# Last group of the FFN down projections as eight plain block products, with the folding of sums, the second down's memory and the first mixer chunk rearranged

## The chip, the cores and the metric

The kernel runs on one core of a Trainium2 chip. It computes one whole decoder layer in one launch. The metric is the device time of that launch in microseconds, as the median of several runs. Engines are called as the profile calls them: PE (TensorE, the matmuls), PEld (its weight loads), DVE (VectorE), ACT (ScalarE), POOL (GpSimd), SP (SyncE, which here only issues DMAs).

## What is computed

The reference is a layer with two half-step feed-forward networks (FFN) around a mixer, cut here to what matters:

```python
def swiglu(x, w_gate, w_up, w_down):
    return (jax.nn.silu(x @ w_gate) * (x @ w_up)) @ w_down

def half_ffn(h, g_pre, g_post, w_gate, w_up, w_down):
    return h + 0.5 * rms_norm(swiglu(rms_norm(h, g_pre), w_gate, w_up, w_down), g_post)
...
h = half_ffn(h, ...)                      # FFN 1
u = rms_norm(h, g_mix_pre); u @ w_in      # mixer: DeltaNet, sliding-window attention, gates
h = h + rms_norm(y @ w_out, g_mix_post)
h = half_ffn(h, ...)                      # FFN 2
```

The model width is 1024, the hidden width 2816 (22 tiles of 128). There are 1040 prompt tokens with the meta tokens and 64 sample tokens: FFN 1 runs over 1104 tokens, FFN 2 over 1088, so half the tokens are 552 and 544. All is in 32-bit floats.

## The kernel before

**Products.** Every float is split into a high and a low part that TensorE can multiply (`hi` and `lo`, in the names `wh`/`wl` and `xh`/`xl`), and a product is three matmuls: high by high, high by low, low by high (the list `FAST`). The two FFNs also use Strassen's scheme in Winograd's form: each of the three matrices is cut in 2 by 2 blocks (tokens in two halves, width in two halves, hidden width in two halves), and seven products of sums of blocks, p = 1 to 7, stand for the eight plain block products.

**Up.** For each pair of hidden tiles f = 0 to 10 (one of each hidden half) gate and up are computed in seven products; `hidden` (L337 to L373) makes from them the silu-gated values `h11, h12, h21, h22` and their sums, splits them, and stores seven slices per f in DRAM (`hid`, by `store`, L369).

**Down** (`Ffn.down`, L445 to L518). The pairs f are taken in groups (0,1), (2,3,4), (5,6), (7,8), (9,10). For each group the four blocks of the weight are loaded (`raw`, L244; ten buffers). For each product p: the operand of the weight is put together by up to two differences on DVE (`T`, L251 and L261) and split by an ACT cast (`wh`, L272) and a POOL subtraction (`wl`, L273), four buffers each; the slice p of `hid` of each f is loaded by SP (`hb`, L480, five buffers); and for each of the four blocks d of 128 output columns PE runs n x 3 x 2 matmuls (n the group's size, 2 the two parts of the tokens, 256 and 296 or 288 columns) into one PSUM buffer `y` (L504), which DVE adds to the accumulator `acc{p}` (L451). For the first group ACT copies it there (L508). There are four PSUM buffers, and two in the last stretch, where the other two are given to the transposes.

**The sums.** The seven accumulators are folded into the four output blocks in the last group: 6+=1, 2+=1, 3+=6, 3+=5, 7+=6, 4+=7, 5+=7, on DVE (L451) and POOL (L452) in turn with the products. Products 7 and 4 come last, in two token parts each. In FFN 1 (`early`) they are done for the last two groups in separate visits at the very end.

**Ends.** `end` (L521, L527) transposes 128 tokens t of the folded blocks to rows: `acc2` and `acc3` for t = 0 to 3, `acc4` and `acc5` for t = 4 to 7, t = 8 being the rest of both. Behind it stands the post norm (L564, L565, with the reciprocal root on POOL, L80, L81) and, in FFN 1, the mixer's pre norm (L96, L98) with its transposes (L102) and their evacuation (L117, L118) to the tiles `uT` of the mixer; in FFN 2 the norm and the store of the output. The ends are woven between the last products, and in FFN 1 also into the mixer's first projections (`m.before`: beta and decay by `ba_steps`, the keys of two heads by `keys_conv`, L745). The mixer's tokens come in chunks of 512, 256 and 336.

**Order.** The code names tiles from pools; a scheduler orders the instructions of each engine by when it expects them to be ready, and each engine then runs its own list in order, waiting on semaphores. SP's list holds nearly all DMAs, so a DMA that waits holds back those listed behind it. A new pool can lie in memory that an earlier one used, and then its first writes wait for the earlier one's last readers. So the memory of the second down (L1958 to L1965, opened after up's pools were closed) decides when its first loads can start.

## Time and profile before

| | |
|---|---|
| Median of 3 runs | 2834.3 us (2832.69 to 2837.92) |
| Profiled execution's own time | 2832.25 us |
| Its span (first to last instruction) | 2830.5 us |
| Mean granted TensorE clock | 0.978 |
| PE busy | 2660.1 us (94%), 18797 instructions |
| PEld busy | 2482.9 us (88%) |
| DVE, ACT, POOL busy | 1657.9, 1106.2, 1417.6 us (59%, 39%, 50%) |
| DMA | 422.55 MB, mean 149 GB/s |

Busy times are shares of the span, averaged over stages that are bound by different things. The stages of this execution, in microseconds from the span's start: first FFN's up until about 517, its down until about 814, the mixer and the merge until about 2135, second FFN's up until 2530.5, its down until 2814, and a tail until 2830.5. A row of the windows view gives for a stretch of time the busy time and the instructions of each engine, the granted clock of TensorE as a share of full speed, and the busy share of the DMA engines. A row of the waits view gives an engine, the operation that waited, what released it, and the total, the number and the longest of such waits.

### The profile page before, as it was taken

How to read it: one execution, taken by the hardware profiler on the slowest of the kernel's cores; microseconds unless marked ns; L12 is line 12 of the kernel's file. 1: busy time of each engine (PE TensorE's matmuls, PEld its weight loads, DVE VectorE, ACT ScalarE, POOL GpSimd, SP SyncE). 2: the span in 40 equal slices, each digit the busy share in tenths (PEclk: the TensorE clock that was granted, in tenths of full speed). 3: DMA queues.
4: the chain of work that ended last, by engine and by line, in shares of the span. 5: the costliest groups of instructions: out<-in, count | busy, mean ns of one | idle time of the engine just before them, and what ended most of it. 6: DMA issues, size and time to landing. Idle time of an engine off the chain costs nothing. (4 is left out here: it accounts for less than half of the span.)

```text
span 2830.5 us, 49313 instructions
## 1 busy us (share of the span) xinstructions
PE 2660.1 (94%) x18797; PEld 2482.9 (88%) x18797; DVE 1657.9 (59%) x2457; ACT 1106.2 (39%) x2599; POOL 1417.6 (50%) x1332
## 2 busy tenths in 40 slices
PE   7999999899878998999999999998999999979996
PEld 6999999899867897887788888887799999979996
DVE  7657656445856669955454444443566665653567
ACT  5334333322255632354444444444533433424122
POOL 6555555444765634644344444444555555544346
PEclk9999999999999999999999999999999999999998
DMA  4344343667743653353333333334434443347664
GB/s 155 130 143 158 126 148 135 244 206 246 240 154 111 216 171 98 95 178 112 91 94 94 94 94 94 94 103 135 157 98 161 146 150 133 144 166 245 224 221 166
DMA packets 234450, 422.55 MB, mean 149 GB/s; under 512 B 60278, under 2 KB 121878, under 8 KB 233926
## 3 DMA queue, kind: packets, MB, share of 16 engines
q1 hardware_dynamic: 213622, 339.72, 37.0%
q10 hardware_dynamic: 20592, 79.68, 7.1%
q8 instruction: 148, 2.42, 0.4%
q14 instruction: 88, 0.72, 0.1%
HBM read 273.71 MB, written 147.27 MB: 149 GB/s over the span
## 5 line engine op out<-in xcount | busy, mean ns | idle before, releaser
L273 POOL TENSOR_TENSOR wl<-T,wh 128x512 fp32r<-128x512 f32 x264 | 351.3, 1340 | 353.6 <-ACT wh L272 181.7
L130 PE MATMUL gu<-xh,wl 128*128 128x256 f32 (+3 forms) x1440 | 496.0, 344 | 0.0
L126 PE MATMUL gu<-xh,wh 128*128 128x256 f32 (+3 forms) x1440 | 491.9, 342 | 0.0
L128 PE MATMUL gu<-xl,wh 128*128 128x256 f32 (+3 forms) x1440 | 491.1, 341 | 0.0
L504 PE MATMUL y<-hb,wh 128*128 128x256 f32 (+2 forms) x2464 | 428.6, 295 | 51.8 <-ACT wh L272 20.3
L273 POOL TENSOR_TENSOR wl<-raw,wh 128x512 fp32r<-128x512 f32 x194 | 266.3, 1380 | 305.5 <-ACT wh L272 219.4
L504 PEld LDWEIGHTS y<-hb,wh 128*128 128x128 f32 x2464 | 362.8, 192 | 58.1 <-ACT wh L272 20.7
L272 ACT CAST wh<-T 128x512 fp32r<-128x512 f32 x264 | 163.2, 620 | 411.4 <-PE y L504 151.8
L130 PEld LDWEIGHTS gu<-xh,wl 128*128 128x128 f32 x1440 | 275.1, 191 | 28.7 <-issue 11.1
L128 PEld LDWEIGHTS gu<-xl,wh 128*128 128x128 f32 x1440 | 275.2, 191 | 20.1 <-issue 1.2
L126 PEld LDWEIGHTS gu<-xh,wh 128*128 128x128 f32 x1440 | 275.7, 191 | 19.1 <-issue 1.6
L504 PE MATMUL y<-hb,wl 128*128 128x256 f32 (+2 forms) x1232 | 266.2, 293 | 9.8 <-POOL wl L273 9.7
L451 DVE TENSOR_TENSOR acc<-acc,y 128x552 f32<-128x552 f32 (+4 forms) x240 | 161.6, 682 | 168.8 <-PE y L504 168.7
L272 ACT CAST wh<-raw 128x512 fp32r<-128x512 f32 x194 | 119.9, 620 | 326.6 <-PE y L504 130.7
L717 POOL TENSOR_TENSOR wl<-raw,wh 128x1024 fp32r<-128x1024 f32 x60 | 145.0, 2416 | 142.7 <-ACT wh L716 121.2
L504 PEld LDWEIGHTS y<-hb,wl 128*128 128x128 f32 x1232 | 205.0, 193 | 11.2 <-POOL wl L273 11.2
L251 DVE TENSOR_TENSOR T<-raw,raw 128x512 f32<-128x512 f32 x136 | 137.1, 1015 | 90.9 <-POOL wl L273 79.3
L261 DVE TENSOR_TENSOR T<-raw,T 128x512 f32<-128x512 f32 x66 | 79.7, 1214 | 79.4 <-POOL wl L273 79.4
L1478 POOL TENSOR_TENSOR f<-f,mhalf 128x1 f32<-128x1 f32 (+1 forms) x72 | 54.6, 758 | 110.9 <-DVE f L1476 103.5
L251 DVE TENSOR_TENSOR T<-raw,T 128x512 f32<-128x512 f32 x70 | 76.5, 1097 | 34.8 <-POOL wl L273 34.6
L869 DVE SCALAR_TENSOR_TENSOR cv<-pc,cw,cv 128x1131 f32<-128x1131 f32 x48 | 69.1, 1442 | 34.2 <-POOL cv L866 33.9
L363 ACT CAST hs<-S 128x552 fp32r<-128x552 f32 (+1 forms) x60 | 39.1, 652 | 116.2 <-DVE S L351 67.0
(585 smaller groups left out, 7489.5 us busy)
## 6 DMA issues: line engine op xcount, KB each, us to landing
hb<-hid SPq DMA_DIRECT2D x77, 552.0 KB
hb<-hid SPq DMA_DIRECT2D x77, 544.0 KB
hid<-hs ACTq DMA_DIRECT2D x70, 552.0 KB
hid<-hs ACTq DMA_DIRECT2D x70, 544.0 KB
raw<-in_w_in_dram SPq DMA_DIRECT2D x58, 512.0 KB
raw<-in_ffn_w_down_dram SPq DMA_DIRECT2D x104, 256.0 KB
raw<-in_ffn_w_gate_dram SPq DMA_DIRECT2D x94, 256.0 KB
raw<-in_ffn_w_up_dram SPq DMA_DIRECT2D x94, 256.0 KB
```

The lines of the kernel that those rows point to most:

```text
L126: nc.tensor.matmul(ps, wh, xh, start=first and i == 0, stop=False)
L128: nc.tensor.matmul(ps, wh, xl, start=False, stop=False)
L130: nc.tensor.matmul(ps, wl, xh, start=False, stop=last and i == n - 1)
L251: self.nc.vector.tensor_tensor(out=b[name], in0=b[x], in1=b[y], op=ALU.subtract)
L261: nc.vector.tensor_tensor(out=s, in0=b["21"], in1=s, op=ALU.subtract)
L272: nc.scalar.copy(hi, s)
L273: nc.gpsimd.tensor_tensor(out=lo, in0=s, in1=f32(hi), op=ALU.subtract)
L451: dve = lambda out, x, y: nc.vector.tensor_tensor(out=out, in0=x, in1=y, op=ALU.add)
L504: nc.tensor.matmul(self.view(ps, (i,)), w[j][x][:, d * P:(d + 1) * P], hb[j][:, y, lo:hi], start=j + x + y == 0, stop=j == n - 1 and x == 1)
L717: nc.gpsimd.tensor_tensor(out=lo, in0=raw, in1=f32(hi), op=ALU.subtract)
L869: nc.vector.scalar_tensor_tensor(out=cv, in0=pc[:, w:w + PADW], scalar=self.cw[:, j, w:w + 1], in1=cv, op0=ALU.mult, op1=ALU.add)
L1478: nc.gpsimd.tensor_tensor(out=f[rows], in0=f[rows], in1=c.mhalf[rows, 0:1], op=ALU.pow)
```

## The change

1. The last group (9,10) is no longer done in seven products but as eight plain block products: output block q of 2, 3, 4, 5 is the sum over four pairs of a plain weight block and a plain slice of `hid` (2 hidden halves, 2 pairs f). The values `h21` become an eighth slice for f = 9 and 10. The four weight blocks of both pairs are split once and kept in `w` and a new pool `w2` (four buffers each). There are no separate visits for products 7 and 4 in FFN 1 any more.
2. The sums of accumulators are issued by `beside` ahead of the plain blocks, in the order of the list `adds`; `acc2` and `acc3` are final first, so that the ends of t = 0 to 3 can run while the blocks of q = 4 and 5 run in token parts.
3. In every group of three, and in one place of the last group, the blocks d = 2 and 3 run together in one turn: each operand is used for both before the next.
4. The load and the cast of the small weights `ba` move from ahead of the first down to behind its second group, by `late_load`.
5. The first two slices that `hidden` stores for each f go through ACT's queue.
6. The mixer's first chunk is projected in two pieces of 256 columns by `ba_steps` and the first two `keys_conv`; the ends are dealt out anew (three streams in `m.before`); chunks 0, 1 and 2 of `uT` have a pool each.
7. The second down's pools are laid out anew, with the raw weights first in the order of loads, six `hb` buffers, and an unused gap; the second up's `x` tiles get a pool per product so that memory comes free product by product.

The core of the diff:

```diff
+    def values(self, hbp, group, p):
+        hb = [self.c.t(hbp, [P, 2, self.half], F32R, tag="hb") for _ in group]
+        for x, f in zip(hb, group):
+            self.nc.sync.dma_start(f32(x), self.h_d[f, p - 1].rearrange("p (x t) -> p x t", x=2))
+        return hb
+
+    def turns(self, ds, items, parts):
+        ps = {}
+        for d in ds:
+            self.psy.append(self.psy.pop(0))
+            ps[d] = self.c.t(self.psy[-1], [P, 1024], tag="y")
+        for j, (w, hb) in enumerate(items):
+            for d in ds:
+                for x, y in FAST:
+                    for i in parts:
+                        lo, hi = self.parts[i]
+                        self.nc.tensor.matmul(self.view(ps[d], (i,)), w[x][:, d * P:(d + 1) * P], hb[:, y, lo:hi],
+                                              start=j + x + y == 0, stop=j == len(items) - 1 and x == 1)
+        for d in ds:
+            yield d, self.view(ps[d], parts)
...
+                for ds in ((0,), (1,), (2, 3)) if len(group) > 2 else ((0,), (1,), (2,), (3,)):
+                    for d, v in self.turns(ds, items, both):
...
+        group = groups[-1]
+        b = self.raw("d", group, ("11", "21", "12", "22"))
+        first = [self.values(hbp, group, p) for p in (1, 2)]
+        w = {name: [self.w_split(self.wp if name[1] == "1" else self.wp2, x[name]) for x in b]
+             for name in ("11", "21", "12", "22")}
+        adds = [[(pool, 6, 1), (dve, 2, 1)], [(dve, 3, 5), (pool, 7, 6)], [(dve, 3, 6)], [(pool, 4, 7)], [(dve, 5, 7)], [], [],
+                []]
...
+        def block(q, column, hb, ds, parts):
+            items = [(x, y) for row, h in zip("12", hb) for x, y in zip(w[row + column], h)]
+            for d, v in self.turns(ds, items, parts):
+                dve(part(q, d, parts), part(q, d, parts), v)
+                yield
...
+        second = [self.values(hbp, group, p) for p in (8, 4)]
+        beside(4)
+        for i in range(2):
+            for q, column in ((4, "1"), (5, "2")):
+                for ds in ((0, 1), (2,), (3,)) if i == 0 and q == 4 else ((0,), (1,), (2,), (3,)):
+                    yield from block(q, column, second, ds, (i,))
...
+        if f in self.plain:
+            split(8, h21)
...
-    c.nc.sync.dma_start(raw, I["w_ba"])
+    late_load(c, raw, I["w_ba"])
...
-        dn = f1.down(GROUPS, accp, hbp, True)
-        drain(steps_of(dn, 28 * len(GROUPS) - 26))
+        dn = f1.down(GROUPS, [(accp, (1, 2, 5, 7, 3, 6, 4))], hbp)
+        drain(steps_of(dn, 28 * 2))
+        ba_w = ba_weights(c, nrm, I)
+        drain(steps_of(dn, 28 * 2))
...
-        weave((steps_of(dn, 8), 0, 1, 8), ends(0, 1))
-        weave((dn, 0, 1, 17), ends((0,), 2, (0,), (1,), 3, (1,), (2,), 4, (2,), (3,), 5, (3,)))
+        weave((dn, 0, 1, 15), ends(0, None, 1, None, None, (0,), (0,), 2, None, (1,), (1,), 3))
...
-        m.before([[ends(6, (4,), (4,), 7, (5,), (5,), 8, (6,), (6,))], [ends((7,), (7,), (8,), (8,))]])
+        m.before([[ends((2,), (2,), 4, (3,), (3,), 5)], [ends((4,), (4,), 6, (5,), (5,), 7, 8)],
+                  [ends((6,), (6,), (7,), (7,), (8,), (8,))]])
...
-        hbp = c.pool(eb, "hb", bufs=5)
+        f2.tp = c.pool(eb, "T", bufs=6)
+        f2.wp2 = c.pool(eb, "w2", bufs=4)
+        acc1 = c.pool(eb, "acc1")
+        c.t(c.pool(eb, "gap"), [P, 896], tag="gap")
+        f2.rawp = c.pool(eb, "raw", bufs=10)
+        f2.wp = c.pool(eb, "w", bufs=4)
+        hbp = c.pool(eb, "hb", bufs=6)
         accp = c.pool(eb, "acc")
-        nrm = c.pool(eb, "nrm", bufs=3)
-        f2.tp = c.pool(eb, "T", bufs=6, side="right")
-        f2.wp = c.pool(eb, "w", bufs=4, side="right")
-        f2.rawp = c.pool(eb, "raw", bufs=10, side="right")
+        nrm = c.pool(eb, "nrm", bufs=3, side="right")
```

At the start of the second down, this is where SP's list stands before the change (`hb` and `hid` are the values, `raw` the weights, `res` the residual rows of the ends):

```order
L480 DMA hb_5090_28398<-hid2_7_71 128x1088
L480 DMA hb_5099_28464<-hid2_7_71 128x1088
L1969 DMA res_5505_30984<-h2_d_5_69 128x1024
L1969 DMA res_5519_31047<-h2_d_5_69 128x1024
L369 DMA hid2_7_71<-hs_5055_28234 128x1088
L1969 DMA res_5526_31085<-h2_d_5_69 128x1024
L369 DMA hid2_7_71<-hs_5056_28239 128x1088
L369 DMA hid2_7_71<-hs_5057_28243 128x1088
L369 DMA hid2_7_71<-hs_5058_28248 128x1088
L244 DMA raw_5067_28304<-in_ffn2_w_down_dram 128x512
```

and where it stands now, from the last weight block of the second up:

```order
L247 DMA raw_4971_28025<-in_ffn2_w_up_dram 128x512
L247 DMA raw_5015_28349<-in_ffn2_w_down_dram 128x512
L247 DMA raw_5016_28351<-in_ffn2_w_down_dram 128x512
L247 DMA raw_5017_28353<-in_ffn2_w_down_dram 128x512
L247 DMA raw_5018_28355<-in_ffn2_w_down_dram 128x512
L247 DMA raw_5021_28361<-in_ffn2_w_down_dram 128x512
L247 DMA raw_5022_28363<-in_ffn2_w_down_dram 128x512
L247 DMA raw_5023_28365<-in_ffn2_w_down_dram 128x512
L247 DMA raw_5024_28367<-in_ffn2_w_down_dram 128x512
L247 DMA raw_5099_28855<-in_ffn2_w_down_dram 128x512
L247 DMA raw_5100_28857<-in_ffn2_w_down_dram 128x512
L458 DMA hb_5019_28357<-hid2_7_71 128x1088
```

The ten first weight loads stood behind the stores of the last hidden values; they now stand right behind the last load of the second up, ahead of all values and of all those stores.

On POOL, in the last group of the second down, before the change:

```order
L452 TENSOR_TENSOR acc6_5061_28298<-acc6_5061_28298,acc1_5060_28297 128x544
L452 TENSOR_TENSOR acc2_5063_28300<-acc2_5063_28300,acc1_5060_28297 128x544
L452 TENSOR_TENSOR acc7_5064_28301<-acc7_5064_28301,acc6_5061_28298 128x256
L452 TENSOR_TENSOR acc7_5064_28301<-acc7_5064_28301,acc6_5061_28298 128x288
L452 TENSOR_TENSOR acc7_5064_28301<-acc7_5064_28301,acc6_5061_28298 128x256
L452 TENSOR_TENSOR acc7_5064_28301<-acc7_5064_28301,acc6_5061_28298 128x288
L452 TENSOR_TENSOR acc7_5064_28301<-acc7_5064_28301,acc6_5061_28298 128x256
L452 TENSOR_TENSOR acc7_5064_28301<-acc7_5064_28301,acc6_5061_28298 128x288
L273 TENSOR_TENSOR wl_5475_30788<-raw_5437_30565,wh_5474_30787 128x512
L273 TENSOR_TENSOR wl_5477_30792<-raw_5438_30567,wh_5476_30791 128x512
```

and after it, from the end of group (7,8), whose last two weights are `wl_5370` and `wl_5372`, into the last group, whose weights of the first column are `wl_5393` to `wl_5399`:

```order
L485 TENSOR_TENSOR acc7_5011_28345<-acc7_5011_28345,acc6_5013_28347 128x544 x3
L279 TENSOR_TENSOR wl_5370_30531<-raw_5299_30100,wh_5369_30530 128x512
L279 TENSOR_TENSOR wl_5372_30535<-raw_5300_30102,wh_5371_30534 128x512
L485 TENSOR_TENSOR acc7_5011_28345<-acc7_5011_28345,acc6_5013_28347 128x544
L485 TENSOR_TENSOR acc4_5010_28344<-acc4_5010_28344,acc7_5011_28345 128x544 x3
L279 TENSOR_TENSOR wl_5393_30625<-raw_5380_30600,wh_5392_30624 128x512
L279 TENSOR_TENSOR wl_5395_30629<-raw_5381_30602,wh_5394_30628 128x512
L485 TENSOR_TENSOR acc4_5010_28344<-acc4_5010_28344,acc7_5011_28345 128x544
L279 TENSOR_TENSOR wl_5397_30633<-raw_5382_30604,wh_5396_30632 128x512
L279 TENSOR_TENSOR wl_5399_30637<-raw_5383_30606,wh_5398_30636 128x512
```

The sums stood between the weight splits of the last group's products; they now stand between those of the group before it, and behind `wl_5399` POOL's list of the last group holds no sum and no split any more.

On PE, where the ends of the second down begin, before (`y` a PSUM buffer of a product, `tr` that of a transpose):

```order
L527 MATMUL tr_5533_31125<-ident_1_62,acc2_5063_28300 128x128 x4
L527 MATMUL tr_5533_31125<-ident_1_62,acc3_5066_28303 128x128 x4
L504 MATMUL y_5538_31145<-hb_5500_30951,wh_5495_30941 128x288 x2
L504 MATMUL y_5538_31145<-hb_5500_30951,wl_5496_30942 128x288
L504 MATMUL y_5538_31145<-hb_5501_30953,wh_5498_30947 128x288 x2
L504 MATMUL y_5538_31145<-hb_5501_30953,wl_5499_30948 128x288
```

and after:

```order
L560 MATMUL tr_5424_30960<-ident_1_62,acc2_5009_28343 128x128 x4
L560 MATMUL tr_5424_30960<-ident_1_62,acc3_5014_28348 128x128 x4
L473 MATMUL y_5429_30980<-hb_5416_30888,wh_5400_30640 128x256 x2
L473 MATMUL y_5429_30980<-hb_5416_30888,wl_5401_30641 128x256
L473 MATMUL y_5429_30980<-hb_5417_30889,wh_5402_30644 128x256 x2
L473 MATMUL y_5429_30980<-hb_5417_30889,wl_5403_30645 128x256
L473 MATMUL y_5429_30980<-hb_5418_30892,wh_5404_30648 128x256 x2
L473 MATMUL y_5429_30980<-hb_5418_30892,wl_5405_30649 128x256
L473 MATMUL y_5429_30980<-hb_5419_30893,wh_5406_30652 128x256 x2
L473 MATMUL y_5429_30980<-hb_5419_30893,wl_5407_30653 128x256
```

Between two blocks that each fill one PSUM buffer there were six matmuls of half the tokens; there are now twelve.

187 lines of the change are left out of this document (84 added, 103 removed).

## The prediction

> **What bounds the kernel now.** I read the page's busy times first, then the windows view for each stage that the change touches, then the waits of PE in the stretches where it idles, then the lists of single engines there. From the page:
>
> ```profile
> PE 2660.1 (94%) x18797; PEld 2482.9 (88%) x18797; DVE 1657.9 (59%) x2457; ACT 1106.2 (39%) x2599; POOL 1417.6 (50%) x1332
> L273 POOL TENSOR_TENSOR wl<-raw,wh 128x512 fp32r<-128x512 f32 x194 | 266.3, 1380 | 305.5 <-ACT wh L272 219.4
> ...
> hb<-hid SPq DMA_DIRECT2D x77, 544.0 KB
> ...
> raw<-in_ffn_w_down_dram SPq DMA_DIRECT2D x104, 256.0 KB
> ```
>
> PE is the bound over the whole, with one split on POOL at 1.38 us, one value of 0.56 MB and one weight of 0.26 MB as the sizes needed below; the question is where PE idles. The windows view (PE busy and matmuls first, granted clock and DMA share last):
>
> ```profile
> 400.00:471.00 71.00, 71.00 (x562) 71.00 (x561) 40.19 (x47) 26.41 (x44) 37.77 (x28) 1.00 0.35 127
> 516.70:550.00 33.30, 22.74 (x163) 22.08 (x162) 21.02 (x23) 10.43 (x20) 15.64 (x11) 0.90 0.67 245
> 550.00:640.00 90.00, 84.08 (x639) 82.92 (x638) 38.07 (x43) 24.95 (x42) 34.66 (x26) 0.98 0.61 210
> 640.00:731.50 91.50, 91.50 (x720) 91.30 (x718) 58.43 (x75) 19.25 (x31) 44.50 (x33) 1.00 0.75 254
> 731.50:852.00 120.50, 93.44 (x631) 83.47 (x630) 81.67 (x101) 52.58 (x88) 78.75 (x87) 0.93 0.51 174
> 2459.00:2530.00 71.00, 71.00 (x569) 71.00 (x568) 34.01 (x44) 24.81 (x41) 36.17 (x27) 1.00 0.27 102
> 2530.00:2560.00 30.00, 10.26 (x63) 9.72 (x62) 14.18 (x21) 6.01 (x10) 8.16 (x6) 0.66 0.98 357
> 2560.00:2657.50 97.50, 92.19 (x724) 90.92 (x723) 41.03 (x44) 32.35 (x54) 40.51 (x32) 1.00 0.64 222
> 2657.50:2762.30 104.80, 104.69 (x832) 104.50 (x832) 69.35 (x88) 21.75 (x35) 48.92 (x38) 1.00 0.65 225
> 2762.30:2814.45 52.15, 40.69 (x286) 38.52 (x287) 37.53 (x52) 10.91 (x20) 36.94 (x39) 0.90 0.50 173
> 2814.45:2830.50 16.05, 3.20 (x24) 2.24 (x22) 10.47 (x12) 4.31 (x11) 5.13 (x8) 0.72 0.37 136
> ```
>
> Up and the middles of both downs are PE without a gap. For the rest I take two losses per row: PE's idle time, and its busy time by (1 - clock), what a lower clock costs while it works. First down: start 10.56 + 2.3 = 12.8, groups to 640 us 5.92 + 1.7 = 7.6, end and mixer start 27.06 + 6.5 = 33.6. Second down: start 19.74 + 3.5 = 23.2, groups 5.3, end 11.46 + 4.1 = 15.5. That is 98 us that the change could reach. Who ends the waits, in the waits view (total, number, longest), stretch by stretch from the start of the first down, its group of three, its end, then the same of the second:
>
> ```profile
> PE y L504 <- ACT acc L508: 9.6, 2, 8.6
> PE y L504 <- DMA hb<-hid: 5.9, 6, 1.9
> PE tr L102 <- ACT res L98: 11.0, 4, 5.6
> PE y L504 <- DVE acc L451: 5.4, 3, 3.6
> PE y L504 <- POOL wl L273: 2.2, 2, 2.0
> PE y L504 <- ACT wh L272: 19.7, 1, 19.7
> PE y L504 <- DMA hb<-hid: 4.5, 5, 1.2
> PE y L504 <- POOL wl L273: 7.5, 3, 5.2
> PE y L504 <- DVE acc L451: 4.1, 4, 2.1
> ```
>
> **The second down's start.** The longest wait names an ACT cast, but ACT had itself waited 23 us for a weight. SP's list issued it behind the values and the last stores, from 2538.88, and the weights came at 2549.5 (start, length, what, number):
>
> ```profile
> 2538.88 11.64 SPq L244 DMA_DIRECT2D raw<-in_ffn_w_down_dram  x10
> 2549.54 1.24 ACT L272 CAST wh<-raw 128x512 fp32r<-128x512 f32 x2 [23.00 <-DMA raw<-in_ffn_w_down_dram]
> ```
>
> And the windows of the same place:
>
> ```profile
> 2505.00:2525.00 20.00, 20.00 (x162) 20.00 (x161) 4.71 (x7) 4.94 (x8) 8.19 (x7) 1.00 0.01 2
> 2535.00:2555.00 20.00, 4.71 (x19) 4.39 (x20) 5.60 (x11) 3.09 (x5) 4.76 (x4) 0.50 1.03 391
> ```
>
> The DMA engines moved nothing for 20 us before and were full for 20 us after. The ten loads now stand ahead of everything; by the waits in the built program their memory comes free 121 matmuls before up ends, 121 x 71.00 / 569 = 15 us, so they are issued from about 2515. Ten weights of 0.26 MB and the first two values of 0.56 MB are 3.7 MB, 9.5 us at the 391 GB/s of the row; the casts and splits (1.24 / 2 = 0.62 and 1.38 us each) run meanwhile. The first product is ready at about 2525, five us before PE comes. Late next are values listed behind the stores of the last hidden slices on SP. I take 2 us as left: a gain of 21. Bounds: 23 if nothing waits, 8 if the full queue only moves and later values come late.
>
> **Groups of three.** With five buffers, a product's third value takes the buffer of the previous product's first, which is free when the last block has done six of its 18 matmuls. A matmul takes 71.00 / 562 = 0.126 us (up's, whose columns are the same), so the buffer is free 12 x 0.126 = 1.5 us before the product ends, and the value is wanted 1.5 us after. The waits' means, 5.9 / 6 and 4.5 / 5, say that it comes 1 us later than that, so such a load takes about 4 us. With two blocks in one turn the first value is done 24 matmuls, 3.0 us, before the end: the 1 us is covered, with 0.5 to spare; in the second down a sixth buffer removes the dependence. Of the 7.6 + 5.3 = 12.9 I leave 2: a gain of 11. Bounds 6 (the longer waits stay) and 12.9.
>
> **The first down's start.** ACT stood 12.41 us before the cast of `ba`, whose load SP had issued late, and PE ran out of PSUM buffers:
>
> ```profile
> 532.41 4.73 SPq L369 DMA_DIRECT2D hid<-hs  x3
> 537.19 0.47 SPq L597 DMA_DIRECT2D baraw<-in_w_ba_dram  x1
> 537.75 1.55 SPq L480 DMA_DIRECT2D hb<-hid  x2
> 542.83 0.30 ACT L599 CAST ba<-baraw 128x128 fp32r<-128x128 f32 x1 [12.41 <-DMA baraw<-in_w_ba_dram]
> ```
>
> That cast goes. Late next is the fourth product's second value, issued at 537.75, landing about when ACT went on (it lands some 6 us after issue in that queue, an estimate between the 4 us of a load above and the 10.7 us from 2538.88 to 2549.54). It still stands behind the stores of the last hidden slices, now with the eighth among them: one more split for ACT and DVE. So the wait only changes its name: I take 0; bounds a gain of 9 (the value comes early) and a loss of 3.
>
> For the two stores that moved to ACT's queue, the row is the 4.73 us for three stores on SP, of which about 3 x 0.33 is issuing and the rest is waiting for DVE. [...]
>
> **The plain group's price.** The group has 8 x 4 x 12 = 384 matmuls in place of 7 x 4 x 12 = 336: 48 more, 48 x 0.126 = 6.1 us in the first down and 48 x 71.00 / 569 = 6.0 in the second. All of it is on the path, since PE is the bound there. [...]
>
> **The first down's end and the mixer's start (731.5 to 852).** The norm chain holds PE for 11.0 us there, the last accumulator adds for 5.4, the splits for 2.2. POOL does the chain's steps, the sums and the splits. From 760 to 790 it is busy 24.78 us by the windows, and its two largest groups there are sums and splits:
>
> ```profile
> 760.00:790.00 30.00, 20.93 (x151) 19.93 (x150) 21.11 (x28) 11.74 (x20) 24.78 (x28) 0.89 0.41 143
> ```
>
> ```profile
> L452 POOL TENSOR_TENSOR acc<-acc,acc 128x256 f32<-128x256 f32 x8 | 7.9, 984 | 1.4 <-DVE acc L451 1.3
> L273 POOL TENSOR_TENSOR wl<-T,wh 128x512 fp32r<-128x512 f32 x4 | 5.1, 1277 | 0.0
> ```
>
> These two, 13.0 of the 24.8 us, leave this stretch: sums and splits stand in the group before, where POOL was busy 44.50 of 91.50 us and so has room for them. The ends of tokens 0 to 3 now have 16 half blocks of 12 matmuls, 24 us, beside them, where blocks had six. What stays is the chain's own latency for tiles that the mixer wants next: two tiles per piece of 256 columns, while a piece gives PE only some 64 matmuls, 8 us. Of 33.6 lost I leave 14, between 5 and 27 (all its idle time as before): a gain of 19.6, less 6.1 and 0.8 of new work, 12.7 net; bounds 22 and 0.
>
> **The second down's end (2762 to 2830).** The POOL waits, 7.5, go with the splits. The adds' 4.1 came where DVE was full:
>
> ```profile
> 2791.40:2814.45 23.05, 18.98 (x134) 17.26 (x133) 22.11 (x32) 6.58 (x12) 13.67 (x19) 0.93 0.68 235
> ```
>
> DVE's 22 us of ends and adds now lie beside 14 half blocks and six transposes, 14 x 1.5 + 6 x 8 x 0.126 = 27 us of PE, so PE leads. Of 15.5 I leave 5: 10.5 less 6.0 is 4.5 net; bounds a gain of 7.5 and a loss of 3.5. The 16 us tail has the same three ends: 0.
>
> **Sum.** 21 + 11 + 0 + 12.7 + 4.5 = 49.2 off the execution's own 2832.25: 2783. The median of the runs is 2 us above that execution, so on its scale 2785.
>
> **Rivals.** *The full DMA queue only moves* (second down's start gains 8, not 21): for it, the 1.03 share for 20 us; against, the idle 20 us before. 2785 + 13 = 2798.
> *The norm chain still binds the first down's end* (27 left, not 14): for it, its 11.0 is the largest wait there; against, POOL's freed 13.0. Also 2798; both, 2811.
> *More goes than I allow*: the first down's value comes early (9), little is left at both ends (8): 2768.
> *Slower: the clock falls in the plain groups.* Their half blocks pass through two PSUM buffers, and PE stops briefly at each if DVE is late. From the windows:
>
> ```profile
> 776.00:784.00 8.00, 4.36 (x22) 4.36 (x23) 3.60 (x5) 2.30 (x3) 6.67 (x8) 0.57 0.16 66
> 790.00:804.00 14.00, 9.64 (x70) 8.28 (x68) 11.82 (x17) 7.21 (x12) 9.62 (x12) 1.00 0.43 149
> ```
>
> At 4.36 of 8 us busy the clock stood at 0.57, at 9.64 of 14 at 1.00. At half clock the two plain groups' 2 x 384 matmuls would take another 2 x 384 x 0.126 = 97 us: 2882. It decides from 55 of these 97 us (49 gained and 5.7) on, that is with half clock through over half of both groups. Against it, short stops at 69% busy cost no clock, and I expect PE busier than that. [...]
>
> **Chances.** Forecast 0.62; the queue moves 0.12; the chain binds 0.12; more goes 0.08; the clock falls 0.06, of which 0.02 come out within 0.2%. A measurement of this kernel can tell about 0.2%, 5.7 us, from no change. Faster 0.94, same 0.02, slower 0.04. The range goes from 2768 (more goes) to 2811 (queue and chain together); the clock's case and part of the ends stay out.
>
> **What would show it.** Right: PE goes from up into the second down with under 3 us idle, its first weights landing before 2525 on the old scale; the waits for values in the groups of three shrink to under 2 us in all; the plain groups show 48 matmuls more each, and no POOL wait in them; PE idles some 10 us less between the last group and the mixer; the first down's start still waits, for a value. Wrong: a granted clock under 0.9 in the plain groups; weights issued only after up's end; waits for values at the second down's start of over 5 us in all; waits of the mixer's first projections for the norm chain of over 20 us.

## The result and the profile after

The changed kernel takes 2798.9 us (median of 4 runs, 2796.8 to 2802.4), the kernel before 2835.4 us (4 runs, 2832.7 to 2837.9): a ratio of 0.987, 95% interval 0.986 to 0.989. It is faster by 36 us (1.3%) where 49 were forecast, and lies inside the range of 2768 to 2811. The profiled execution has a span of 2795.0 us against 2830.5. From its page:

```profile
PE 2669.6 (96%) x18957; PEld 2502.6 (90%) x18957; DVE 1619.9 (58%) x2415; ACT 1099.8 (39%) x2592; POOL 1390.0 (50%) x1296
```

PE runs 160 matmuls more and is busy 9.5 us longer, and yet the span is 35.5 us shorter. To say where, both spans are cut at the same matmuls, counted from the first product of each down (the group (0,1) has 336, the group of three 504), and at the first matmul of the mixer's decay, which comes after its first projections ("fold"). Stage lengths in us, from the traces:

| Stage | Forecast change | Before | After | Change |
|---|---|---|---|---|
| first up and all ahead of it | 0 | 516.9 | 516.0 | -0.8 |
| first down, group (0,1) | 0 | 55.5 | 54.5 | -1.0 |
| first down, group of three | -6 | 73.1 | 64.3 | -8.8 |
| first down, next 672 matmuls | 0 | 85.5 | 85.5 | 0.0 |
| first down's last group, to the fold | -12.7 | 121.0 | 119.8 | -1.2 |
| mixer, merge, second up | 0 | 1678.7 | 1683.4 | +4.7 |
| second down, from up's end, group (0,1) | -21 | 64.6 | 49.1 | -15.5 |
| second down, group of three | -5 | 70.0 | 62.7 | -7.3 |
| second down, next 672 matmuls | 0 | 84.4 | 83.6 | -0.8 |
| second down's last group, and the tail | -4.5 | 81.0 | 76.1 | -4.8 |

The windows view of the changed kernel for these stages (the first row is the first down's group (0,1), then its group of three, its last group, the way on to the fold, and for the second down the group (0,1), the group of three and the last group; PE busy first, granted clock and DMA share last):

```profile
516.03:570.50 54.47, 45.31 (x337) 44.65 (x336) 28.74 (x30) 23.53 (x41) 25.44 (x17) 0.94 0.69 250
570.50:634.79 64.29, 64.29 (x507) 64.17 (x506) 29.35 (x39) 13.86 (x24) 30.02 (x23) 1.00 0.73 239
720.26:779.04 58.78, 54.93 (x428) 53.75 (x427) 31.10 (x44) 13.37 (x23) 17.03 (x19) 1.00 0.38 131
779.04:840.01 60.97, 46.28 (x321) 42.83 (x319) 27.15 (x29) 34.46 (x61) 28.56 (x39) 0.86 0.36 120
2523.44:2572.50 49.06, 43.90 (x337) 43.24 (x336) 26.62 (x31) 22.69 (x41) 18.24 (x14) 0.97 0.87 343
2572.50:2635.22 62.72, 62.72 (x507) 62.72 (x505) 30.19 (x39) 13.58 (x23) 29.24 (x22) 1.00 0.74 242
2718.84:2778.99 60.15, 56.95 (x436) 56.07 (x435) 34.65 (x46) 8.21 (x16) 11.60 (x16) 0.94 0.35 121
```

Both groups of three are now PE without a gap. The two last groups are nearly so. But behind the first one PE idles 14.7 of 61 us at a clock of 0.86. What ends PE's waits, in the waits view, from the first down's start, then from its last group to the fold (five rows), then the second down's start and its last group:

```profile
PE y L473 <- DMA hb<-hid: 8.1, 2, 7.4
...
PE tr L104 <- ACT res L100: 8.4, 2, 5.8
PE tr L104 <- ACT acc L100: 5.4, 2, 2.8
PE y L473 <- POOL wl L279: 2.3, 2, 1.6
PE y L473 <- DMA hb<-hid: 1.5, 2, 1.1
PE tr L104 <- DVE xl L120: 0.6, 1, 0.6
...
PE y L473 <- ACT acc L512: 5.1, 2, 4.1
...
PE y L473 <- POOL wl L279: 3.2, 2, 2.5
```

Of the waits that were quoted of before, the 19.7 us for the first weight and all eleven for values in the groups of three are gone. The first down's start still waits, for a value instead of ACT: 9.1 us in all with 1.0 for ACT, 10.5 before. The norm chain is at 8.4 + 5.4 = 13.8; before it was 11.0, and 13.3 with the 2.3 us that PE's transposes waited for its step on DVE (L564). So the chain's waits have not become shorter. One wait is new: 5.1 us for ACT's copies in the second down's start. And the waits for weight splits, which were to go, are 2.3 us (2.2 before) and 3.2 us (7.5 before) in the plain groups.

### The profile page after: what moved, and what is told of

Same layout as the page of the kernel before. It is cut to its first block, busy times and chain, and to the rows that moved or that the text cites. A ratio compares the mean times of both kernels' runs of the same rounds, so it can differ in the third digit from the quotient of the medians.

```text
span 2795.0 us, 49454 instructions
## 1 busy us (share of the span) xinstructions
PE 2669.6 (96%) x18957; PEld 2502.6 (90%) x18957; DVE 1619.9 (58%) x2415; ACT 1099.8 (39%) x2592; POOL 1390.0 (50%) x1296
## 5 line engine op out<-in xcount | busy, mean ns | idle before, releaser
L132 PE MATMUL gu<-xh,wl 128*128 128x512 f32 (+3 forms) x1456 | 502.8, 345 | 0.1
L279 POOL TENSOR_TENSOR wl<-T,wh 128x512 fp32r<-128x512 f32 x248 | 338.3, 1370 | 326.7 <-ACT wh L278 237.0
L128 PE MATMUL gu<-xh,wh 128*128 128x512 f32 (+3 forms) x1456 | 498.5, 342 | 0.0
L130 PE MATMUL gu<-xl,wh 128*128 128x512 f32 (+3 forms) x1456 | 497.4, 342 | 0.0
L473 PEld LDWEIGHTS y<-hb,wh 128*128 128x128 f32 x2528 | 370.1, 190 | 18.1 <-DMA hb<-hid 10.5
L128 PEld LDWEIGHTS gu<-xh,wh 128*128 128x128 f32 x1456 | 281.8, 194 | 18.6 <-issue 1.6
L278 ACT CAST wh<-T 128x512 fp32r<-128x512 f32 x248 | 153.3, 621 | 349.0 <-PE B L305 109.0
L473 PE MATMUL y<-hb,wl 128*128 128x256 f32 (+2 forms) x1264 | 274.5, 291 | 5.5 <-POOL wl L279 5.5
L484 DVE TENSOR_TENSOR acc<-acc,y 128x552 f32<-128x552 f32 (+4 forms) x216 | 144.9, 679 | 154.3 <-PE y L473 153.8
L254 DVE TENSOR_TENSOR T<-raw,raw 128x512 f32<-128x512 f32 x124 | 118.7, 960 | 105.5 <-POOL wl L279 102.6
L264 DVE TENSOR_TENSOR T<-raw,T 128x512 f32<-128x512 f32 x62 | 70.9, 1146 | 67.9 <-POOL wl L279 67.8
L254 DVE TENSOR_TENSOR T<-raw,T 128x512 f32<-128x512 f32 x62 | 65.6, 1064 | 32.1 <-POOL wl L279 31.9
```

Of the source, the lines that this page charges most:

```text
L128: nc.tensor.matmul(ps, wh, xh, start=first and i == 0, stop=False)
L130: nc.tensor.matmul(ps, wh, xl, start=False, stop=False)
L132: nc.tensor.matmul(ps, wl, xh, start=False, stop=last and i == n - 1)
L254: self.nc.vector.tensor_tensor(out=b[name], in0=b[x], in1=b[y], op=ALU.subtract)
L264: nc.vector.tensor_tensor(out=s, in0=b["21"], in1=s, op=ALU.subtract)
L278: self.nc.scalar.copy(hi, s)
```

## The experiments

The theory after this reading: the load order and the pairing did what the forecast says; what fell short are the first down's end, where the norm chain and not the sums and splits is the bound, and two small stalls: the new one for ACT's copies, and the one for weight splits that stayed. The rivals: the full DMA queue bounds the second down's start; the plain group costs more than it saves; the 4.7 us in code that did not change are a price of the change. Each experiment but the last two alters one part of the changed kernel. The median of the kernel before lies between 2835.0 and 2837.8 us from one group of runs to the next, so the stages of the profiles decide, and the ratio to the kernel before stands beside them (0.987 for the changed kernel).

**The second down's memory as before** (`old_mem2`):

```diff
-        f2.tp = c.pool(eb, "T", bufs=6)
-        f2.wp2 = c.pool(eb, "w2", bufs=4)
-        acc1 = c.pool(eb, "acc1")
-        c.t(c.pool(eb, "gap"), [P, 896], tag="gap")
-        f2.rawp = c.pool(eb, "raw", bufs=10)
-        f2.wp = c.pool(eb, "w", bufs=4)
         hbp = c.pool(eb, "hb", bufs=6)
         accp = c.pool(eb, "acc")
-        nrm = c.pool(eb, "nrm", bufs=3, side="right")
+        nrm = c.pool(eb, "nrm", bufs=3)
+        f2.wp2 = c.pool(eb, "w2", bufs=4, side="right")
+        f2.tp = c.pool(eb, "T", bufs=6, side="right")
+        f2.wp = c.pool(eb, "w", bufs=4, side="right")
+        f2.rawp = c.pool(eb, "raw", bufs=10, side="right")
...
-        dn = f2.down(GROUPS, [(acc1, (1,)), (accp, (2, 4, 7, 5, 6, 3))], hbp)
+        dn = f2.down(GROUPS, [(accp, (1, 6, 5, 2, 7, 4, 3))], hbp)
```

The accumulators go back to their old order in one pool with it.

> The changed kernel with the second down's pools laid out as before (raw weights again in memory that the second up still uses), six value buffers kept. Stage measured: from the end of up to the 337th matmul of the second down, 64.6 us in the kernel before and 49.1 in the changed one. If the place of the ten weight loads is the cause, the first weight lands some 20 us after up's end again, PE idles 18 to 22 us there, the stage is 63 to 68 us and the whole is 14 to 20 us slower than the changed kernel. If the full DMA queue is the bound whatever the order, the stage stays within 5 us of 49 and the whole within 5 us.

Measured: stage 69.6 us, median 2823.5 us, ratio 0.995 (0.994 to 0.997); both are somewhat worse than the first theory says. SP's list in the changed kernel, and under it in this one:

```profile
2508.32 5.92 SPq L247 DMA_DIRECT2D raw<-in_ffn_w_down_dram  x10
2514.29 5.30 SPq L458 DMA_DIRECT2D hb<-hid  x6
```

```profile
2527.85 2.94 SPq L458 DMA_DIRECT2D hb<-hid  x6
2531.57 12.19 SPq L376 DMA_DIRECT2D hid<-hs  x6
2543.82 2.37 SPq L2005 DMA_DIRECT2D res<-h_d  x3
2546.61 13.30 SPq L247 DMA_DIRECT2D raw<-in_ffn_w_down_dram  x12
```

```profile
PE y L473 <- DMA raw<-in_ffn_w_down_dram: 25.3, 1, 25.3
```

Up ends at 2523.4 in the one and at 2528.0 in the other: the loads start 15 us ahead of its end or 18.6 us behind it, and PE waits 25.3 us for them in the second case. Inside the changed kernel the place of the loads is worth 20.6 us of stage; against the kernel before, whose loads began 8.3 us behind up's end, the stage gained 15.5. That is the cause, and not the full queue alone.

**The second down's accumulators in another order** (`acc_order`):

```diff
-        dn = f2.down(GROUPS, [(acc1, (1,)), (accp, (2, 4, 7, 5, 6, 3))], hbp)
+        dn = f2.down(GROUPS, [(acc1, (1,)), (accp, (2, 6, 5, 7, 4, 3))], hbp)
```

> The changed kernel with the accumulators of the second down in another order of memory (2, 6, 5, 7, 4, 3), so that the two that are written last lie on the buffers of the last hidden values' stores. If the one new stall of 4.1 us in the second down's start is ACT waiting to overwrite a buffer whose store is still in the DMA queue, that stall and the half clock behind it (1.6 us) go: the stage from up's end to the 337th matmul falls from 49.1 to 43 to 45 us and the whole is 4 to 6 us faster than the changed kernel. If the full queue is the bound, PE waits for a value in its place and the stage stays at 48 to 50 us.

The stall that it aims at, on ACT in the changed kernel, and PE's waits in this one:

```profile
2552.38 1.64 ACT L512 COPY acc<-y 128x544 f32<-128x544 f32 x3 [7.17 <-DMA hid<-hs]
```

```profile
PE y L473 <- ACT acc L512: 1.0, 1, 1.0
PE y L473 <- DMA hb<-hid: 0.5, 2, 0.2
```

Measured: stage 44.2 us, 4.9 less. `acc6`, written from the fourth product on, lay over the buffer of a hidden slice whose store was still under way: SP had issued it at 2543.44, and the DMA engines were full until ACT went on (share 1.03). ACT waited 7.2 us for that store to have read the buffer, the four PSUM buffers filled up, and PE stopped. The median is 2798.0, no better than the changed kernel's (ratio 0.987, 0.984 to 0.989): this profile took 6.6 us more in the mixer, the merge and the second up, where the code is the same, which `before_again` takes up. So the gain of this edit alone is seen in its stage, not in the median.

**The pairing undone** (`pair_off`):

```diff
-                for ds in ((0,), (1,), (2, 3)) if len(group) > 2 else ((0,), (1,), (2,), (3,)):
+                for ds in ((0,), (1,), (2,), (3,)):
```

The two pairs of blocks in the last group stay as they are.

> The changed kernel with every group of three done block by block again (the last two blocks not in one turn). The 504 matmuls of the group of three take 73.1 us in the first and 70.0 in the second down of the kernel before, 64.3 and 62.7 in the changed one. If the wait for the third value hangs on the moment its buffer is freed, the waits come back in the first down, which has five buffers (72 to 74 us there), and not in the second, which has six (62 to 64): 7 to 10 us slower in all. If the pairing itself removed the waits in both, both come back and the whole is 14 to 18 us slower.

Measured: 72.0 us in the first down, 62.7 in the second, as the first theory has it; median 2804.6, ratio 0.989 (0.987 to 0.991). PE's waits in the first group of three:

```profile
PE y L473 <- DMA hb<-hid: 6.4, 6, 2.5
```

In the first down the pairing hides the third value's wait; in the second the waits stay away without it. That they do so by the sixth buffer is argued from the count of buffers: no run gives that down five buffers in the new layout. Six waits of 6.4 us in all lengthen the stage by 7.7 (PE is busy 65.6 us in place of 64.3): each costs some 0.2 us beyond its idle time.

**The second down's last group in seven products** (`seven2`), with the code of the kernel before for this down:

```diff
-        dn = f2.down(GROUPS, [(acc1, (1,)), (accp, (2, 4, 7, 5, 6, 3))], hbp)
+        dn = f2.down7(GROUPS, [(acc1, (1,)), (accp, (2, 4, 7, 5, 6, 3))], hbp, False)
...
-        weave((dn, 0, 1, 15), (f2.tail_steps(ptr, nrm, finish2, (0, 1, 2, None, 3, None, 4, 5)), 0.05, 0.95, 8))
+        weave((dn, 0, 1, 17), (f2.tail_steps(ptr, nrm, finish2, (0, 1, 2, 3, 4, 5)), 0.05, 0.95, 6))
```

> The changed kernel with the second down's last group in seven products and its sums between them, as in the kernel before; all the rest stays, and no eighth slice is stored in the second FFN. Stage measured: from the 1513th matmul of the second down to the end, 81.0 us in the kernel before and 76.2 in the changed one. If the splits and sums on POOL cost more there than 48 matmuls (6 us), POOL waits of about 7 us and 4 us of waits for DVE come back, the stage is 79 to 83 us and the whole 3 to 7 us slower than the changed kernel. If the price of the 48 matmuls is the larger, the stage is 70 to 75 us and the whole 2 to 6 us faster.

```profile
PE y L607 <- POOL wl L279: 7.6, 3, 5.2
PE y L607 <- DVE acc L554: 3.9, 4, 2.1
```

Measured: stage 80.6 us against 76.1; the waits of before are back (7.5 and 4.1 us there). The plain group is worth 4.5 us here. By the windows view the last group lost 11.5 us of idle time and 53.4 x 0.08 = 4.3 us of clock in the kernel before (2749.50 to 2814.43), 3.2 and 57.0 x 0.06 = 3.4 in the changed one: 9 us less, against 4 us that PE is busy longer, at full clock, with 48 matmuls more. The median is 2810.6, ratio 0.991 (0.990 to 0.993), more than the stage says, because the second down's start also takes longer, 55.8 against 49.1 us. SP's list and PE's wait there:

```profile
2515.78 5.46 SPq L583 DMA_DIRECT2D hb<-hid  x6
2521.79 12.07 SPq L247 DMA_DIRECT2D raw<-in_ffn_w_down_dram  x10
```

```profile
PE y L607 <- ACT wh L278: 8.7, 1, 8.7
```

With the old code the ten weight loads stand behind six values again and begin 3 us ahead of up's end (2524.9), ACT waits 12.0 us for a weight, and PE for its cast: the same cause as in `old_mem2`, in a smaller dose.

**The sums 7+=6 and 4+=7 on DVE** (`sums_dve`):

```diff
-        adds = [[(pool, 6, 1), (dve, 2, 1)], [(dve, 3, 5), (pool, 7, 6)], [(dve, 3, 6)], [(pool, 4, 7)], [(dve, 5, 7)], [], [],
+        adds = [[(pool, 6, 1), (dve, 2, 1)], [(dve, 3, 5), (dve, 7, 6)], [(dve, 3, 6)], [(dve, 4, 7)], [(dve, 5, 7)], [], [],
```

> The changed kernel with the sums 7+=6 and 4+=7 on DVE instead of POOL, in both downs. If POOL's sums ahead of the last group's weight splits make PE wait for the splits (2.3 us in the first down, 3.2 us and 2.9 us of half clock in the second), those waits go: the stage from the 1513th matmul to the end of the second down's products falls from 60.2 to 54 to 57 us, in the first down by 2 to 3 us. If DVE's list then delays its adders of the PSUM buffers, PE waits for DVE instead and the stages stay within 1.5 us.

POOL in the changed kernel, where the second down's last group begins at 2718.8 (its first splits `wl` are the second row's, and the next two the fourth's):

```profile
2711.75 5.81 POOL L485 TENSOR_TENSOR acc<-acc,acc 128x544 f32<-128x544 f32 x4
2717.52 3.50 POOL L279 TENSOR_TENSOR wl<-raw,wh 128x512 fp32r<-128x512 f32 x2
2720.98 1.82 POOL L485 TENSOR_TENSOR acc<-acc,acc 128x544 f32<-128x544 f32 x1
2722.78 3.46 POOL L279 TENSOR_TENSOR wl<-raw,wh 128x512 fp32r<-128x512 f32 x2
```

With the edit, PE's only wait in the second down's last group is this one:

```profile
PE y L473 <- POOL wl L279: 0.5, 1, 0.5
```

Measured: the second down's last group 54.2 us in place of 60.2: 2.7 us of waits less, and the rest is about what the clock of 0.94 cost the changed kernel there (57.0 x 0.06 = 3.4 us). In the first down it is 58.6 against 58.8, not the 2 to 3 us less that were expected: the waits for splits (2.3 us) are gone, and what took their place was not shown. Median 2788.4, ratio 0.983 (0.981 to 0.985). Sums put ahead of a split that PE wants at once cost 5.9 us here.

**The first down as before** (`seven1`): seven products with separate visits for 7 and 4, the old ends, whole chunks.

```diff
-        dn = f1.down(GROUPS, [(accp, (1, 2, 5, 7, 3, 6, 4))], hbp)
+        dn = f1.down7(GROUPS, [(accp, (1, 2, 5, 7, 3, 6, 4))], hbp, True)
...
-        weave((dn, 0, 1, 15), ends(0, None, 1, None, None, (0,), (0,), 2, None, (1,), (1,), 3))
+        weave((steps_of(dn, 8), 0, 1, 8), ends(0, 1))
+        weave((dn, 0, 1, 17), ends((0,), 2, (0,), (1,), 3, (1,), (2,), 4, (2,), (3,), 5, (3,)))
```

> The changed kernel with the first down as in the kernel before: last groups in seven products with separate visits for 7 and 4, its sums among them, the old dealing of ends, whole chunks in the mixer's start (and so no pairing in its group of three, which alone costs 7.7 us by an earlier run). Stage measured: from the 1513th matmul of the first down to the first matmul of the mixer's decay (the fold), 121.0 us in the kernel before and 119.8 in the changed one. If the plain group there only trades its waits for its own matmuls and for the norm chain's waits, the stage stays within 2 us of 120 and the whole is 6 to 10 us slower than the changed kernel, all of it in the group of three. If the changed kernel's other parts had hidden a real gain there, the stage is 130 us or more.

```profile
PE tr L104 <- ACT res L100: 10.8, 3, 5.6
PE y L607 <- DVE acc L554: 4.3, 5, 2.1
...
PE y L607 <- POOL wl L279: 2.3, 2, 2.0
```

Measured: 122.7 us to the fold, the group of three 71.0; median 2808.3, ratio 0.989 (0.986 to 0.992). Six kernels that do not touch the first down's end or the mixer's start lie between 118.4 and 123.0 us there (in the changed kernel, at 119.8, half clock takes 46.3 x 0.14 = 6.5 us of it), so 122.7 is no difference: taken together, what the first down's end was rebuilt for moved nothing that these runs can tell.

**Whole chunks with four ends early** (`whole`), and **pieces with four ends early** (`ends_early`):

```diff
-PIECES = ((0, 0, 256), (0, 256, 256)) + WHOLE[1:]
+PIECES = WHOLE
...
-        weave((dn, 0, 1, 15), ends(0, None, 1, None, None, (0,), (0,), 2, None, (1,), (1,), 3))
+        weave((dn, 0, 1, 15), ends(0, 1, (0,), (0,), 2, (1,), (1,), 3, (2,), (2,), (3,), (3,)))
```

> The changed kernel with the mixer's first chunk in one piece of 512 columns and two streams of ends, four tiles' ends finished beside the plain blocks. If the pieces are what lets the mixer start ahead of the norm chain, PE waits longer for tiles 2 and 3 before its first projection: the stage from the 1513th matmul to the fold rises from 119.8 to 124 to 132 us. If the norm chain's own rate is the bound, the stage stays within 2 us of 120.

> The changed kernel with pieces kept, and the ends of tiles 2 and 3 finished beside the plain blocks instead of in the mixer's first stream; tiles 4 to 8 follow one stream earlier. If PE's waits of 13.8 us for the norm chain there come from ends that are begun too late, the stage from the 1513th matmul to the fold falls from 119.8 to 108 to 114 us. If ACT, DVE and POOL are then full beside the blocks, the waits move to the blocks and the stage stays at 117 to 124 us.

In `ends_early` the first line (`PIECES`) stays as in the changed kernel and the streams of `m.before` begin with tiles 4 and 5. Measured: 122.8 and 123.9 us; medians 2803.3 and 2802.0, both ratios 0.987 (0.985 to 0.989). PE's waits for the chain, `whole` first:

```profile
PE tr L104 <- ACT res L100: 9.3, 4, 4.5
PE tr L104 <- ACT acc L100: 4.7, 1, 4.7
```

```profile
PE tr L104 <- ACT res L100: 8.1, 4, 3.5
PE tr L104 <- ACT acc L100: 6.2, 3, 4.3
```

14.0 and 14.3 us, against 13.8: dealt out earlier or later, in one piece or two, PE waits as long for the chain. What is saved behind the last group is lost in it (the last group takes 70.9 and 71.8 us in place of 58.8).

**The first two input weights split on DVE** (`win_dve`):

```diff
-        self.ready = {8 + h: self.w_in(8 + h, self.nc.scalar) for h in range(2)}
+        self.ready = {8 + h: self.w_in(8 + h, self.nc.scalar, self.nc.vector) for h in range(2)}
```

> The changed kernel with the two first input weights' low parts made by DVE instead of POOL (4.7 us on POOL at 780.6, ahead of a norm step that was ready at 782.6 and ran at 785.3). If that delay makes PE's longest wait there (5.8 us), it falls to 2 to 4 us, with less half clock behind it, and the stage from the 1513th matmul to the fold falls by 3 to 6 us. If another step is as late, the wait stays and the stage changes by less than 1.5 us.

POOL in the changed kernel, ahead of PE's longest wait (5.8 us, until 792.2):

```profile
780.57 4.74 POOL L752 TENSOR_TENSOR wl<-raw,wh 128x1024 fp32r<-128x1024 f32 x2 [1.04 <-ACT wh L751]
785.28 0.19 POOL L82 TENSOR_SCALAR rp<-rp 128x1 f32<-128x1 f32 x1
```

The norm step behind the two splits was ready at 782.6. With the edit POOL runs it then, and PE's waits are these:

```profile
782.69 0.19 POOL L82 TENSOR_SCALAR rp<-rp 128x1 f32<-128x1 f32 x1 [3.24 <-ACT dump L81]
```

```profile
PE tr L104 <- ACT res L100: 8.1, 2, 4.2
PE tr L560 <- DVE xl L120: 3.5, 1, 3.5
PE tr L104 <- ACT acc L100: 2.8, 2, 2.1
```

Measured: 115.9 us, 3.8 less than the changed kernel and below all six of the others; median 2795.8, ratio 0.985 (0.983 to 0.987). PE's longest wait fell from 5.8 to 4.2 us, since the norm step no longer stands behind two wide splits on POOL: that much of the chain's delay was theirs. Not all of the 3.8 us is the chain's. Its waits went from 13.8 to 10.9 and 3.5 came in for DVE, while the 2.3 us for weight splits stayed away in this run. All of PE's waits there are 1.7 us less (16.7 against 18.4); what the rest of the 3.8 is was not shown.

**All last stores through ACT** (`store_act`):

```diff
-        def store(queue=nc.sync if f == NF // 2 - 1 else nc.scalar):
+        def store(queue=nc.scalar):
```

> The changed kernel with all of the last pair's hidden slices stored through ACT's queue, so that no store stands before a value on SP. If the fourth product's second value comes late in the first down because it is listed behind those stores (PE waited 7.4 us for it), it is issued some 4 to 7 us earlier and the stage from up's end to the 337th matmul of the first down falls from 54.5 to 47 to 51 us; ACT's own issues cost at most 8 x 0.33 us. If the full DMA queue is what makes it late, whichever list it stands in, the stage stays at 53 to 56 us.

```profile
529.78 9.45 ACTq L376 DMA_DIRECT2D hid<-hs  x4
539.27 2.19 ACT L512 COPY acc<-y 128x552 f32<-128x552 f32 x4 [10.78 <-DMA hid<-hs]
```

```profile
PE y L473 <- ACT acc L512: 17.1, 1, 17.1
```

Neither theory: the stage is 61.7 us in the first down and 56.5 in the second, 7 longer in each; median 2813.6, ratio 0.993 (0.991 to 0.994). Four stores stood 9.5 us on ACT's list, and ACT's copies out of PSUM behind them, which waited 10.8 us. The run does not decide between the two theories, since ACT became the bound. The trace of the changed kernel says more: PE stopped at 537.4, and the value was issued at 540.17, right behind the last store on SP's list, issued at 539.75. For the stores SP had waited on DVE, which made their slices:

```profile
SPq L376 <- DVE hs L358: 8.1, 4, 4.0
```

PE went on at 544.8. The value's own buffer (five, taken in turn) was the second product's, which PE had left at 529.4. So its place on the list made it late: 2.8 us of PE's 7.4 passed before it was issued at all. What an earlier issue would have gained in the full queue (DMA share 0.96 from 531 to 545) no run shows. (The stores of all other pairs go through ACT's queue in every kernel here, the one before too: item 5 of the change moves two stores of the last pair alone, and this edit its other six.)

**The kernel before, once more** (`before_again`), for the stages that did not change:

> The kernel before, unchanged, profiled once more. The mixer, the merge and the second up are the same code in both kernels, yet took 1678.7 us in the profile before and 1683.4 us in that of the changed one, with 21 and 29 us lost to half clock. If that is chance from execution to execution (eight variants of the changed kernel lie between 1680 and 1690), this profile shows them at 1680 to 1690 too; if the change costs 4.7 us there, it shows 1677 to 1680.

Measured: 1684.4 us for mixer, merge and second up, 5.7 more than in the first profile of the same kernel; span 2835.7. So the 4.7 us by which the changed kernel was longer there lie within what two profiles of one kernel differ by. All other stages agree with the first profile within 1.4 us, but for the first group of three (70.6 against 73.1). The second up shows how the chance works, in the windows view of the second up of `ends_early`, the changed kernel and `acc_order`, which have the same code there:

```profile
2042.92:2525.08 482.16, 473.62 (x3767) 471.60 (x3766) 288.67 (x346) 188.30 (x319) 268.75 (x197) 1.00 0.40 144
```

```profile
2039.05:2523.44 484.39, 476.27 (x3767) 474.44 (x3766) 288.25 (x346) 188.19 (x319) 267.37 (x197) 0.99 0.40 143
```

```profile
2047.19:2534.11 486.92, 478.64 (x3767) 476.81 (x3766) 288.49 (x346) 188.12 (x319) 267.26 (x197) 0.98 0.40 143
```

The idle time is 8.1 to 8.5 us in all three; the granted clock differs, and the length with it, in steps of 2.2 and 2.5 us. The kernel before, profiled twice, took 482.5 and 484.2 us there.

**The three edits that paid, together** (`three`): `acc_order`, `sums_dve` and `win_dve` in one kernel.

> The changed kernel with three of the edits together: the second down's accumulators in the other order of memory, the sums 7+=6 and 4+=7 on DVE, the two first input weights' low parts on DVE. If the three act on separate stalls, as their stages say (4.9, 5.9 and 3.8 us), the second down's start is 44 us, its end 54 us, the first down's end and mixer's start 115 to 118 us, and the whole is about 14 us faster than the changed kernel, some 2780 to 2790 us. If DVE, which now holds all of it, becomes the one that PE waits for, one of the three stages stays where it was and the whole is 2788 us or more.

Measured: 2785.5 us (5 runs, 2780.3 to 2789.6), ratio 0.981 (0.980 to 0.983). The three stages are 44.3, 54.2 and 115.2 us. They act on separate stalls. PE's waits from the first down's last group to the fold:

```profile
PE tr L104 <- ACT res L100: 7.7, 2, 4.2
PE tr L104 <- ACT acc L100: 4.9, 2, 2.8
PE y L473 <- DMA hb<-hid: 2.3, 3, 1.0
```

The chain is still the bound there, with 12.6 us. The version is 13 us faster than the changed kernel and 51 faster than the kernel before.

## Why the prediction was right, and where it was not

- **The second down's start** (forecast 21, measured 15.5). Right in its mechanism: the loads stand ahead of up's end, PE goes on without a wait, and undoing it alone brings 20.6 us back. The step that failed is the one on what is late next: "values listed behind the stores of the last hidden slices on SP", with 2 us left. Late next was an accumulator laid over a slice that a store had not yet read. It cost 4.9 us where 2 were left in the sum, and `acc_order` takes it away.
- **Groups of three** (forecast 11, measured 16.1). Right: `pair_off` shows the pairing's part in the first down; that the sixth buffer does the same in the second is argued, not shown alone. The size was off because I left 2 us of waits where none stayed, and counted idle time and clock, where a wait costs a little more than its idle time (0.2 us more each in `pair_off`); and the first group of three in the profile before was 2.5 us longer than in the second profile of it.
- **The first down's start** (forecast 0, measured -1.0). Right: the wait changed its name from ACT to a value behind the last stores, as said, 7.4 us.
- **The first down's end** (forecast 12.7, measured 1.2). This step failed. I took 13 of POOL's 24.8 us as what slowed the norm chain and left 14 of 33.6 us lost. Left were, in the windows above, 3.9 + 14.7 us of idle time and 46.3 x 0.14 = 6.5 us of clock, 25 in all. The chain's waits did not shrink (13.3 us before with DVE's step, 13.8 now); what was gained in other waits paid for the matmuls that were added. No run shows the 0.8 us that the sum takes for new work besides the 6.1; `ends_early`, with the pieces of 256 columns, took 1.1 us more to the fold than `whole`, without them (123.9 against 122.8), less than the 4.6 us by which kernels with the same code differ there. The rival "the norm chain still binds", at 27 left, is what happened. `sums_dve` has two of POOL's three sums on DVE and still 12.6 us of waits for the chain, `whole` and `ends_early` show that the dealing of the ends did not move it, `seven1` that all of it together did not, and `win_dve` that POOL did hold one step of the chain, for 1.6 us of PE's time, but with other work.
- **The second down's end** (forecast 4.5, measured 4.8). Right in sum. But "no POOL wait" was wrong: 3.2 us of waits and 6.83 us at half clock behind them, from sums put ahead of the first splits, 5.9 us as `sums_dve` shows. I had read from the order that the sums stand in the group before, and not asked whether the last of them still fit ahead of the splits. Without them the gain would have been twice as large (4.8 + 5.9).
- **The clock rival.** The clock stood at 1.00 and 0.94 in the plain groups, so the swing that it needs did not come. These rows hardly test it: PE idled 3.9 of 58.8 and 3.2 of 60.2 us, and the 0.94 is one stretch of 6.83 us at half clock, from 2723.46, begun within the wait for the first splits (2.5 us, until 2724.57); `sums_dve`, with 0.5 us of that wait left, is 6.0 us shorter there. The clock did fall, to 0.86, where PE idled a quarter of the time (14.7 of 61 us) behind the first of them.
- **The queue rival.** DMA was nearly full in the second down's start (share 0.87 over 49 us), and still only the one stall came of it (5.1 us).
- **The total.** 2798.9 us is, to within 1 us, what the forecast gives if either of two rivals holds alone. That closeness is partly luck: the first down's end fell 11.5 short as the norm chain's rival says, while the second down's start fell 5.5 short and the unchanged code took 4.7 more by chance, against 5.1 more than forecast from the groups of three.

## What to carry to other kernels

When a stage is bound by a chain of small steps across engines, taking other work off one of those engines moves the stage only if that work was what the chain waited for: read the step that was ready and did not run, and what stood ahead of it. Here two sums taken off POOL left 12.6 us of waits for the chain, and two splits taken off it cut the longest from 5.8 to 4.2 us. Memory laid out anew brings its own waits, and they show under the name of whoever writes first (5.1 us under ACT's copies here); order the tiles so that the last written lie on the last read (4.9 us in `acc_order`). Work moved "beside" other work has to be placed against the next thing that the bound engine wants, not only into a stretch with room in it (5.9 us in `sums_dve`).

## What the runs showed of the hardware that was not expected

The same code with nearly the same idle time (8.1 to 8.5 us) took 482.2, 484.4 or 486.9 us in the second up, at a granted clock of 1.00, 0.99 and 0.98 (`ends_early`, the changed kernel, `acc_order`). In the changed kernel the clock stood at half there for 10.2 us, in three stretches of 3.41 us from 2047.62, 2078.34 and 2122.71; in the first profile of the kernel before, with 482.5 us, for one such stretch. In these two traces the last stretch at half clock lasts 12.11 and 11.03 us; of the 44 others 26 last 3.41 us, 17 last 6.83 us and one 20.48 us. Why nearly the same idle time (8.1 and 8.7 us) goes with three such stretches in one execution and with one in another was not shown. Over the mixer, merge and second up together, where PE runs 10897 matmuls, the profiles lay between 1678.7 and 1690 us, so single profiles can't settle a few us in the sum, whereas a stage without gaps repeated: the first 336 matmuls behind the first down's group of three took 42.70 us before and after.

A store on ACT's list cost more here than its issue, which takes 0.33 us where nothing holds it (the changed kernel at 2519.91): in `store_act` four of them stood there for 9.5 us, most likely since the slices that they store were not ready (in the changed kernel SP waited 8.1 us for DVE to make them), ACT's copies out of PSUM stood behind them, and PE waited 17.1 us. What stands behind the store in that engine's list was the larger part of its price in this run.
